# Weight sums by subtraction and by an accumulating DMA, low halves last, and one block summed in PSUM, in a two-layer trunk

## The chip, the cores and the metric

The kernel runs on one core of a Trainium2 chip. The metric is the device time of one launch in microseconds (us). The kernel before took 1077.22 us, the median of three runs (1075.41, 1077.22 and 1082.15). The five engines of the core, TensorE (PE), VectorE (DVE), ScalarE (ACT), GpSimd (POOL) and SyncE (SP), each work through a list of instructions in order and wait for each other by semaphores. DMAs are issued from SP's and POOL's lists.

## The reference

The model has two layers on an input of 512 rows by 1024 columns, all float32. Each layer has three groups of attention-like heads behind one projection, and then a feed-forward part; only the latter is touched here:

```python
    x = x + jnp.concatenate([ya, yb, yc], axis=-1) @ w_out
    u = _rms(x, norm2) @ w_ff1
    return x + jnp.square(jax.nn.relu(u)) @ w_ff2
```

`w_ff1` is 1024 by 4096 and `w_ff2` 4096 by 1024.

## The kernel before

**Products of split numbers.** Each float32 weight block is split into a high half, written by ScalarE (`whi`, L203), and a low half, which VectorE gets as the block less its high half (`wlo`, L204). The activations are split alike. A matmul pair then becomes three: high by high, high by low, low by high (`mm3`, L260 to 263). Splits of weights go through three buffer pairs (`HIB = 3`), so a split can start when the product three back has been read out by TensorE.

**Seven products for eight.** The feed-forward part of a layer (L1090 to 1343) runs the first two of eight ff1 row groups plainly (`ff1_std`), and the other six in a Strassen/Winograd form (`ff1_st`, L1219): the weight is cut into blocks A11, A12, A21, A22, and seven products are made with A11, S1 = A21 + A22, S2 = S1 + A11, A12, S4 = S2 + A12, S3 = A11 + A21 and A22, in the order A11, S1, S2, A12, S4, S3, A22 (L47; signs are put into the stored blocks). ff2 does the same in eight groups (`ff2`, L1277): four steps s with two column halves dg each, whose products alternate. Here ff1 groups are called a2 to a7, ff2 groups b0.0, b0.1, b1.0, to b3.1. `ff_pairs` (L117) interleaves them one by one: a b product, then an a product, for 84 products; the last 14 are b products alone (b3.0 and b3.1). A b group so has its own next product four products later and an a group two later, and in the last 14 a b group's is two later. Each product is 24 matmuls of 128 by 128 weights with 256 moving columns.

**Operands.** Weights are loaded into 128x1024 buffers, three `raw` and four `fraw`, handed out in rings in the order of the products (`load_ahead`, `take`, `drop`): a load can start when an earlier job gives its buffer back. A one-block operand is a plain DMA from SP's list (L156). For the sums of two blocks from HBM (S1 and S3), SP loads the first and POOL issues a DMA that adds the second while it is written (L158). S2 and S4 are summed by VectorE into A11's buffer (L214, L218).

**Outputs.** `ff1_st` adds products in PSUM banks and by VectorE: block (0,0) is the first product, which ScalarE copies to the SBUF tile `ct`, plus another product, added by VectorE (L1233). ScalarE then makes relu squared in `ct`; `csplit`, `gsplit`, `n1_`, `n2_` and `tail_` (L1164 to 1190) form the sums and splits of the activations that ff2 needs, in the tiles `gx`, `yg`, `xhl`. `acc` (L1257) adds each ff2 product from its bank into the running sum `xT` (L1265).

**What sets the order.** The code states the work in the order of the products; the framework's scheduler then puts each engine's instructions in a fixed order, weighing when it believes each one to be ready. So the place of an instruction in an engine's list isn't that of its line in the code, and a wait in the list holds up all that stands behind it.

Of the kernel before, what the change touches and what calls it, by code (L numbers as in the profile page):

```python
# [15 lines left out]
AF = mybir.ActivationFunctionType  # L16
ALU = mybir.AluOpType
AX = mybir.AxisListType

P = 128  # L20
# [30 lines left out]
def trunk(ctx, tc, x, cols, rows, gate_w, tabs, w_in, w_out, w1, w2, out):  # L51
    nc = tc.nc
    V, A, G, T = nc.vector, nc.scalar, nc.gpsimd, nc.tensor
# [31 lines left out]
    def wt(tag, name):  # L85
        n, bufs = phase["tags"][tag]
        return phase["pool"].tile([P, n], F32, tag=tag, name=nm(name), bufs=bufs)
# [4 lines left out]
    def smt(n, name):  # L92
        return sm.tile([P, n], F32, tag=f"sm{n}", name=nm(name))

    def v3(a, d=HD):
        return a.rearrange("p (h d) -> p h d", d=d)
# [12 lines left out]
    def st_group(l, blocks):  # L109
        grp = {}  # L110
        for which, ij in (("A11", ((0, 0),)), ("S1", ((1, 0), (1, 1))), ("S2", ()), ("A12", ((0, 1),)), ("S4", ()),
                          ("S3", ((0, 0), (1, 0))), ("A22", ((1, 1),))):
            grp[which] = {"ap": [blocks[i, j] for i, j in ij], "which": which, "grp": grp, "n": 4, "w": 256, "ff": l,
                          "gate": None, "parts": 1}
        return grp
# [51 lines left out]
    def drop(jb):  # L167
        jb["ring"].append(jb.pop("raw"))
# [12 lines left out]
    def hilo():  # L181
        hi = wp.tile([P, D], F32R, tag="whi", name=nm("whi"), bufs=HIB)
        lo = wp.tile([P, D], F32R, tag="wlo", name=nm("wlo"), bufs=HIB)
        return hi, lo

    def prep_part(jb, part):
        if "hl" not in jb:
            jb["hl"] = hilo()
        hi, lo = jb["hl"]
        n, w, raw = jb["n"], jb["w"], jb["raw"]  # L190
        W = w
        if jb["gate"] is not None:
            l, k0 = jb["gate"]
            W = 268
            h3, l3, r3 = v3(hi[:, :n * W], W), v3(lo[:, :n * W], W), v3(raw[:, :n * w], w)
            A.activation(h3[:, :, :w], r3, AF.Copy)
            V.tensor_copy(h3[:, :, w:], gws[l][0][:, k0:k0 + n, :])
            V.tensor_tensor(l3[:, :, :w], r3, h3[:, :, :w], ALU.subtract)
            V.tensor_copy(l3[:, :, w:], gws[l][1][:, k0:k0 + n, :])
        else:  # L200
            m = n * w // jb["parts"]
            cs_ = slice(part * m, (part + 1) * m)
            A.activation(hi[:, cs_], raw[:, cs_], AF.Copy)  # L203
            V.tensor_tensor(lo[:, cs_], raw[:, cs_], hi[:, cs_], ALU.subtract)  # L204
        if part == jb["parts"] - 1:
            jb["res"] = [(hi[:, q * W:(q + 1) * W], lo[:, q * W:(q + 1) * W]) for q in range(n)]
            if jb["which"] in (None, "S3", "A22"):
                drop(jb)

    def prep_job(jb):  # L210
        which, g = jb["which"], jb.get("grp")
        if which == "S2":
            a = jb["raw"] = g["A11"]["raw"]
            V.tensor_tensor(a, g["S1"]["raw"], a, ALU.add)  # L214
            drop(g["S1"])
        elif which == "S4":
            a = jb["raw"] = g["A11"]["raw"]
            V.tensor_tensor(a, g["A12"]["raw"], a, ALU.add)  # L218
            drop(g["A12"])
        for part in range(jb["parts"]):  # L220
            prep_part(jb, part)
        if which == "S4":
            drop(g["A11"])

    def prep_ahead(i):
        while pos["prep"] < len(jobs):
# [11 lines left out]
    def getjob():  # L238
        i = pos["get"]
        if i > 0:  # L240
            jobs[i - 1].pop("res", None)
        load_ahead(i)
        prep_ahead(i)
        pos["get"] += 1
        return jobs[i]["res"]
# [14 lines left out]
    def mm3(o, sh, sl, mh, ml, first, last, skip=False):  # L260
        T.matmul(o, sh, mh, start=first, stop=False, skip_group_check=skip)  # L261
        T.matmul(o, sh, ml, start=False, stop=False, skip_group_check=skip)  # L262
        T.matmul(o, sl, mh, start=False, stop=last, skip_group_check=skip)  # L263
# [132 lines left out]
    def headrms(zt, nh, name):  # L396
        sq = wt("tmp", "hsq")
        A.activation(sq[:, :nh * HD], zt, AF.Square)
        ss = smt(nh, name)
        V.tensor_reduce(ss, v3(sq[:, :nh * HD]), AX.X, ALU.add)  # L400
        v = smt(nh, name + "v")
# [42 lines left out]
    for l in range(L):  # L444
        last = l == L - 1
# [288 lines left out]
        def runA():  # L734
# [7 lines left out]
            def s1(c):  # L742
# [8 lines left out]
                for r in range(2):  # L751
                    V.tensor_reduce(v3(mx, 2)[:, :, r], v3(sc[r], 256)[:, :, :nk], AX.X, ALU.max)
                nmx = smt(4, "nmx")
# [321 lines left out]
        ct, bt = 0, 0  # L1075
# [19 lines left out]
        ct = v3(wt("ct", "ct"), S)  # L1095
# [11 lines left out]
        def bank():  # L1107
            return banks.popleft()
# [16 lines left out]

        def prod(bk, bh, bl, start):
            ws = getjob()
            for kk in range(4):
                hi, lo = ws[kk]
                for f in range(2):  # L1130
                    c = slice(f * P, (f + 1) * P)
                    mm3(bk[:, f * 256:(f + 1) * 256], hi[:, c], lo[:, c], bh(kk), bl(kk), start and kk == 0 and f == 0,
                        kk == 3 and f == 1, True)

        def prod1(bk, op, start=True):
            bh, bl = xop(op, 0), xop(op, 1)
            prod(bk, lambda kk: bh[:, kk, :], lambda kk: bl[:, kk, :], start)
# [37 lines left out]
        def act(a, src, sign):  # L1175
            A.activation(ct[:, a], src, AF.Relu, scale=sign)
            A.activation(ct[:, a], ct[:, a], AF.Square)
# [39 lines left out]
                    yield  # L1217

        def ff1_st(s, rr):  # L1219
            X = bank()  # L1220
            prod1(X, 0)
            A.activation(ct[:, 0], X, AF.Copy)
            yield
            Z = bank()
            prod1(Z, 3)
            A.activation(ct[:, 3], Z, AF.Copy)
            yield
            prod1(X, 4, False)
            A.activation(ct[:, 1], X, AF.Copy)
            yield  # L1230
            Y = bank()
            prod1(Y, 1)
            V.tensor_tensor(ct[:, 0], Y, ct[:, 0], ALU.add)  # L1233
            banks.append(Y)
            act(0, ct[:, 0], 1.0)
            csplit(s, rr)
            yield
            prod1(Z, 2, False)
            V.tensor_tensor(ct[:, 1], Z, ct[:, 1], ALU.add)
            banks.append(Z)  # L1240
            act(1, ct[:, 1], 1.0)
            n1_()
            yield
            prod1(X, 5, False)
            V.tensor_tensor(ct[:, 3], X, ct[:, 3], ALU.add)
            act(3, ct[:, 3], -1.0)
            n2_(s, rr)
            yield
            prod1(X, 6, False)
            act(2, X, -1.0)  # L1250
            banks.append(X)
            tail_(s, rr)
            yield
# [23 lines left out]
        def ff2(s):  # L1277
# [18 lines left out]
            for dg in range(2):  # L1296
                Y = bank()
                prod2(Y, s, 1)
                acc(s, dg, 0, 0, Y, True)
                banks.append(Y)  # L1300
# [102 lines left out]
```

## Time and profile before

| | |
|---|---|
| three runs | 1075.41, 1077.22, 1082.15 us |
| profiled execution | 1074.93 us, its span 1073.2 us |
| TensorE (PE) busy | 1059.1 us, 99% |
| VectorE (DVE) busy | 911.9 us, 85% |
| ScalarE (ACT) busy | 626.4 us, 58% |
| GpSimd (POOL) busy | 103.8 us, 10% |
| read from HBM | 147.86 MB |
| accumulating DMAs issued by POOL for weights | 56 |

The span is the time from the first to the last instruction in the trace; the time of the run is a little longer. In a row of the groups by line stand the line, the engine, the operation, the tile written and the tiles read, the count, then busy time and the mean of one in ns, and then the idle time just before and what ended it. In a row of the timeline stand start, duration (both in us), engine, line and operation, and in brackets the idle time ahead of it. A row of the waits has the total in us, how many, and the longest. In the chain a row has its start and its share of the time up to the next piece. The instructions of TensorE overlap each other, so their starts tell the pace, not their durations; the same goes for VectorE, where one starts about 0.08 us before the end of the one ahead.

### The profile page before, as it was taken

How to read it: one execution, taken by the hardware profiler on the slowest of the kernel's cores; microseconds unless marked ns; L12 is line 12 of the kernel's file. 1: busy time of each engine (PE TensorE's matmuls, PEld its weight loads, DVE VectorE, ACT ScalarE, POOL GpSimd, SP SyncE). 2: the span in 40 equal slices, each digit the busy share in tenths (PEclk: the TensorE clock that was granted, in tenths of full speed). 3: DMA queues.
4: the chain of work that ended last, by engine and by line, in shares of the span. 5: the costliest groups of instructions: out<-in, count | busy, mean ns of one | idle time of the engine just before them, and what ended most of it. 6: DMA issues, size and time to landing. Idle time of an engine off the chain costs nothing.

```text
span 1073.2 us, 20903 instructions
## 1 busy us (share of the span) xinstructions
PE 1059.1 (99%) x8376; PEld 989.8 (92%) x8376; DVE 911.9 (85%) x1550; ACT 626.4 (58%) x1097; POOL 103.8 (10%) x154
## 2 busy tenths in 40 slices
PE   8999999999999999999999999999999999999998
PEld 8999977887999999999999998778789999999998
DVE  6696877899997997988977878688999889799897
ACT  5446655376666566566454567444765665576662
POOL 2030020101010010010001200101000100000100
PEclk8999999999999999999999999999999999999999
DMA  6533121145478588588435321213334866876872
GB/s 200 164 110 109 59 68 50 62 174 118 118 197 215 140 213 209 149 210 223 108 108 155 102 80 41 86 44 136 112 87 141 233 178 172 219 183 191 211 185 99
DMA packets 47346, 151.81 MB, mean 141 GB/s; under 512 B 5632, under 2 KB 8832, under 8 KB 47248
## 3 DMA queue, kind: packets, MB, share of 16 engines
q1 hardware_dynamic: 39184, 121.10, 33.8%
q0 software_dynamic: 8064, 29.36, 16.2%
q8 instruction: 66, 1.08, 0.4%
q14 instruction: 32, 0.26, 0.1%
HBM read 147.86 MB, written 2.13 MB: 140 GB/s over the span
## 4 chain that ended last, share of the span: by engine, by line
PE 80%; DVE 11%; ACT 3%; DMA 3%; issue 1%; SPq 0%; DVEq 0%; POOLq 0%
PE at L261 24%; PE at L263 24%; PE at L262 24%; DMA raw<-in_w_dram 3%; DVE wlo L204 2%; DVE rt L719 2%; PE at L849 1%; PE at L891 1%; PE at L874 1%; ACT whi L203 1%; ACT pe L762 1%; PE at L972 1%; DVE yg L1168 1%; DVE z L715 1%; DVE z L721 1%
## 5 line engine op out<-in xcount | busy, mean ns | idle before, releaser
L203 ACT ACTIVATE whi<-raw 128x1024 fp32r<-128x1024 f32 (+1 forms) x144 | 150.9, 1048 | 143.7 <-PE at L262 103.2
L204 DVE TENSOR_TENSOR wlo<-raw,whi 128x1024 fp32r<-128x1024 f32 (+1 forms) x144 | 173.8, 1207 | 41.2 <-ACT whi L203 40.7
L203 ACT ACTIVATE whi<-fraw 128x1024 fp32r<-128x1024 f32 x122 | 129.2, 1060 | 92.4 <-PE at L262 76.2
L261 PE MATMUL at<-yg,whi 128*128 128x256 f32 (+1 forms) x592 | 179.8, 307 | 0.0
L263 PE MATMUL at<-yg,wlo 128*128 128x256 f32 (+1 forms) x592 | 178.4, 301 | 0.0
L262 PE MATMUL at<-xhl,whi 128*128 128x256 f32 (+1 forms) x576 | 177.9, 309 | 0.0
L262 PE MATMUL at<-yg,whi 128*128 128x256 f32 (+1 forms) x560 | 169.6, 303 | 0.0
L261 PE MATMUL at<-whi,xhl 128*128 128x256 f32 (+1 forms) x576 | 164.1, 285 | 2.1 <-ACT whi L203 1.3
L262 PE MATMUL at<-wlo,xhl 128*128 128x256 f32 (+1 forms) x576 | 161.5, 280 | 0.3 <-DVE wlo L204 0.3
L263 PE MATMUL at<-whi,xhl 128*128 128x256 f32 (+1 forms) x576 | 161.5, 280 | 0.0
L261 PE MATMUL at<-xhl,whi 128*128 128x256 f32 (+1 forms) x512 | 161.1, 315 | 0.0
L263 PE MATMUL at<-xhl,wlo 128*128 128x256 f32 (+1 forms) x512 | 160.3, 313 | 0.0
L204 DVE TENSOR_TENSOR wlo<-fraw,whi 128x1024 fp32r<-128x1024 f32 x122 | 148.9, 1221 | 8.6 <-ACT whi L203 8.1
L261 PEld LDWEIGHTS at<-yg,whi 128*128 128x128 f32 x592 | 111.2, 188 | 5.6 <-issue 1.7
L263 PEld LDWEIGHTS at<-yg,wlo 128*128 128x128 f32 x592 | 111.2, 188 | 5.3
L262 PEld LDWEIGHTS at<-xhl,whi 128*128 128x128 f32 x576 | 108.0, 188 | 7.6 <-issue 0.5
L261 PEld LDWEIGHTS at<-whi,xhl 128*128 128x128 f32 x576 | 109.4, 190 | 3.2 <-ACT whi L203 1.6
L262 PEld LDWEIGHTS at<-wlo,xhl 128*128 128x128 f32 x576 | 109.5, 190 | 0.5 <-DVE wlo L204 0.5
L263 PE MATMUL at<-xbx,wlo 128*128 128x256 f32 x384 | 106.6, 278 | 3.4 <-DVE wlo L204 3.4
L263 PEld LDWEIGHTS at<-whi,xhl 128*128 128x128 f32 x576 | 109.3, 190 | 0.3 <-DVE xhl L328 0.3
L262 PEld LDWEIGHTS at<-yg,whi 128*128 128x128 f32 x560 | 105.3, 188 | 4.2 <-DVE yg L1002 0.5
L261 PE MATMUL at<-xbx,whi 128*128 128x256 f32 x384 | 106.1, 276 | 0.0
(286 smaller groups left out, 2423.1 us busy)
## 6 DMA issues: line engine op xcount, KB each, us to landing
fraw<-in_w_dram SPq DMA_DIRECT2D x90, 512.0 KB, 4.5
raw<-in_w_dram SPq DMA_DIRECT2D x66, 512.0 KB, 4.5
raw<-in_w_in_dram SPq DMA_DIRECT2D x34, 512.0 KB, 3.4
fraw<-in_w_dram POOLq DMA_DIRECT2D x34, 512.0 KB, 6.0
raw<-in_w_dram POOLq DMA_DIRECT2D x22, 512.0 KB, 7.9
raw<-in_w_out_dram SPq DMA_DIRECT2D x16, 512.0 KB, 3.4
rowb<-drow SPq DMA_DIRECT2D x16, 256.0 KB, 4.0
raw<-in_w_in_dram SPq DMA_DIRECT2D x12, 256.0 KB, 3.8
```

Source lines behind the costliest of these rows:

```text
L203: A.activation(hi[:, cs_], raw[:, cs_], AF.Copy)
L204: V.tensor_tensor(lo[:, cs_], raw[:, cs_], hi[:, cs_], ALU.subtract)
L261: T.matmul(o, sh, mh, start=first, stop=False, skip_group_check=skip)
L262: T.matmul(o, sh, ml, start=False, stop=False, skip_group_check=skip)
L263: T.matmul(o, sl, mh, start=False, stop=last, skip_group_check=skip)
L715: V.tensor_tensor(z10, z10, bc(rq), ALU.mult)
L719: V.tensor_tensor(r10[:, oo:oo + n, a:a + 32], z10[:, oo:oo + n, b:b + 32], tb(S_, n, a, a + 32), ALU.mult)
L721: V.tensor_tensor(zaq[t], ro[:, :640], rt[:, :640], ALU.add)
L762: A.activation(pe[:, u, :nk], sc[u % 2][:, (u // 2) * 256:(u // 2) * 256 + nk], AF.Exp, bias=nmx[:, u:u + 1], accum_out=ssum[:, u:u + 1])
L849: T.matmul(sp[:, :nk], qTB[rs, pr, n * P:(n + 1) * P], kTB[rs, pr, :nk], start=True, stop=False)
L874: T.transpose(pt[:, b * P:(b + 1) * P], scs[r][:, b * P:(b + 1) * P], ident)
L891: T.matmul(pobs[pr][r * 64:(r + 1) * 64, n * P:(n + 1) * P], zbv[b][:, h * 64:(h + 1) * 64], ps[r][:, b * P:(b + 1) * P], start=b == 0, st ...
```

## The change

- S3 is formed as S2 - A22: only A22 is loaded, and VectorE subtracts it from S2 in A11's buffer (L222). A22's own product then uses the buffer already loaded, with no load.
- S4 is formed in A12's buffer: when A12 has been split, POOL issues an accumulating DMA from SBUF to SBUF (L229) that adds S2 to it. No VectorE sum is left for S4.
- A product (`prod`) runs its 16 matmuls with the high halves first (with the high and the low half of the moving side), then the 8 with the low halves. Before, the three kinds alternated.
- Block (0,0) of `ff1_st` is summed in PSUM: ScalarE copies the first product's bank X to a bank Y, and the other product accumulates there. The VectorE add is gone; Y is held from the group's start.

```diff
-                          ("S3", ((0, 0), (1, 0))), ("A22", ((1, 1),))):
+                          ("S3", ((1, 1),)), ("A22", ())):
...
-        n, w, raw = jb["n"], jb["w"], jb["raw"]
+        n, w, raw = jb["n"], jb["w"], jb.get("src", jb.get("raw"))
...
-            if jb["which"] in (None, "S3", "A22"):
+            if jb["which"] is None:
                 drop(jb)
...
     def prep_job(jb):
         which, g = jb["which"], jb.get("grp")
-        if which == "S2":
-            a = jb["raw"] = g["A11"]["raw"]
-            V.tensor_tensor(a, g["S1"]["raw"], a, ALU.add)
-            drop(g["S1"])
-        elif which == "S4":
-            a = jb["raw"] = g["A11"]["raw"]
-            V.tensor_tensor(a, g["A12"]["raw"], a, ALU.add)
-            drop(g["A12"])
+        last = None
+        if which:
+            a = g["A11"].get("raw")
+            jb["src"] = a if which in ("S2", "S3") else jb["raw"] if "raw" in jb else None
+            if which == "S2":
+                V.tensor_tensor(a, g["S1"]["raw"], a, ALU.add)
+                drop(g["S1"])
+            elif which == "S4":
+                jb["src"], last = g["A12"]["raw"], g["A12"]
+            elif which == "S3":
+                V.tensor_tensor(a, a, jb["raw"], ALU.subtract)
+                last = g["A11"]
+            elif which == "A22":
+                jb["src"], last = g["S3"]["raw"], g["S3"]
         for part in range(jb["parts"]):
             prep_part(jb, part)
-        if which == "S4":
-            drop(g["A11"])
+        if which == "A12":
+            nc.gpsimd.dma_start(jb["raw"], a, accum_op=ALU.add)
+        if last:
+            drop(last)
...
             ws = getjob()
-            for kk in range(4):
-                hi, lo = ws[kk]
-                for f in range(2):
-                    c = slice(f * P, (f + 1) * P)
-                    mm3(bk[:, f * 256:(f + 1) * 256], hi[:, c], lo[:, c], bh(kk), bl(kk), start and kk == 0 and f == 0,
-                        kk == 3 and f == 1, True)
+            for i in range(2):
+                for kk in range(4):
+                    for f in range(2):
+                        c, o = slice(f * P, (f + 1) * P), bk[:, f * 256:(f + 1) * 256]
+                        w = ws[kk][i][:, c]
+                        T.matmul(o, w, bh(kk), start=start and i == kk == f == 0, stop=i == 1 and kk == 3,
+                                 skip_group_check=True)
+                        if i == 0:
+                            T.matmul(o, w, bl(kk), start=False, stop=False, skip_group_check=True)
...
     def ff1_st(s, rr):
-            X = bank()
+            X, Y = bank(), bank()
             prod1(X, 0)
-            A.activation(ct[:, 0], X, AF.Copy)
+            A.activation(Y, X, AF.Copy)
...
-            Y = bank()
-            prod1(Y, 1)
-            V.tensor_tensor(ct[:, 0], Y, ct[:, 0], ALU.add)
+            prod1(Y, 1, False)
+            act(0, Y, 1.0)
             banks.append(Y)
-            act(0, ct[:, 0], 1.0)
```

The change moves instructions on VectorE. Two places follow. The first is where b1.0 begins in layer 0 (with a4): `wlo_630` is the low half of b1.0's A11, `wlo_632` of a4's A11, `wlo_634` of b1.1's A11; `raw1_74` holds b1.0's A11. Lines from L210 on have other numbers after the change (L1183, L1184, L1168 and L1265 are L1194, L1195, L1179 and L1274). Before:

```order
L204 TENSOR_TENSOR wlo_630_4138<-raw1_74,whi_629_4137 128x1024 [waits DMAHW5_50,DVE_50,Activation_50]
L1183 SCALAR_TENSOR_TENSOR ct_527_2865<-ct_527_2865 128x512 [waits DVE_50,Activation_50]
L1184 TENSOR_TENSOR ct_527_2865<-ct_527_2865 128x512
L1265 TENSOR_TENSOR xT_89<-xT_89,at_544_2964 128x2x256 [waits PE_50]
L204 TENSOR_TENSOR wlo_632_4168<-fraw_528_2866,whi_631_4167 128x1024 [waits DMAHW4_50,Activation_50]
L1168 TENSOR_TENSOR gx_526_2864<-ct_527_2865,gx_526_2864 128x1024 [waits Activation_50]
L214 TENSOR_TENSOR fraw_528_2866<-fraw_528_2866 128x1024 [waits DMASW0_50,DVE_50]
L204 TENSOR_TENSOR wlo_634_4203<-fraw_528_2866,whi_633_4202 128x1024 [waits DMAHW6_50,PE_50,Activation_50]
L214 TENSOR_TENSOR raw1_74<-raw2_75,raw1_74 128x1024 [waits DMASW1_50]
```

And now:

```order
L204 TENSOR_TENSOR wlo_630_4132<-raw1_74,whi_629_4131 128x1024 [waits DMAHW0_50,DVE_50,Activation_50]
L217 TENSOR_TENSOR raw1_74<-fraw_528_2866,raw1_74 128x1024 [waits DMASW1_50,DVE_50]
L1194 SCALAR_TENSOR_TENSOR ct_527_2865<-ct_527_2865 128x512 [waits Activation_50]
L1195 TENSOR_TENSOR ct_527_2865<-ct_527_2865 128x512
L1274 TENSOR_TENSOR xT_89<-xT_89,at_545_2965 128x2x256 [waits PE_50]
L1179 TENSOR_TENSOR gx_526_2864<-ct_527_2865,gx_526_2864 128x1024 [waits Activation_50]
L204 TENSOR_TENSOR wlo_632_4162<-fraw_528_2866,whi_631_4161 128x1024 [waits DMAHW1_50]
L204 TENSOR_TENSOR wlo_634_4197<-fraw_528_2866,whi_633_4196 128x1024 [waits DMAHW2_50,PE_50,Activation_50]
```

The S2 sum of b1.0, which waits for POOL's accumulating DMA of S1 (DMASW1), stood behind three splits and now stands behind the first of them. The same holds for b2.0 and for both groups in layer 1.

The second place is S4 of a4, in layer 0. `wlo_644` is the low half of a4's A12, `wlo_646` of b1.0's S2, `wlo_648` of a4's S4. Before, with the sum for S4 of a4 in the first row and that of b1.0 (L218, `raw1_74`) in the fifth:

```order
L218 TENSOR_TENSOR fraw_528_2866<-raw0_73,fraw_528_2866 128x1024 [waits DMAHW2_50,DVE_50]
L1265 TENSOR_TENSOR xT_89<-xT_89,at_541_2961 128x2x256 [waits PE_50]
L204 TENSOR_TENSOR wlo_644_4351<-raw0_73,whi_643_4350 128x1024 [waits Activation_50]
L204 TENSOR_TENSOR wlo_646_4381<-raw1_74,whi_645_4380 128x1024 [waits PE_50,Activation_50]
L218 TENSOR_TENSOR raw1_74<-raw2_75,raw1_74 128x1024 [waits DMAHW4_50,DVE_50]
L1265 TENSOR_TENSOR xT_89<-xT_89,at_542_2962 128x2x256 [waits PE_50]
L204 TENSOR_TENSOR wlo_648_4412<-fraw_528_2866,whi_647_4411 128x1024 [waits Activation_50]
```

And now:

```order
L1274 TENSOR_TENSOR xT_89<-xT_89,at_542_2962 128x2x256 [waits PE_50]
L204 TENSOR_TENSOR wlo_644_4344<-raw2_75,whi_643_4343 128x1024 [waits DMAHW6_50,Activation_50]
L204 TENSOR_TENSOR wlo_646_4375<-raw1_74,whi_645_4374 128x1024 [waits PE_50,Activation_50]
L222 TENSOR_TENSOR fraw_528_2866<-fraw_528_2866 128x1024 [waits DMAHW0_50,DMASW3_50]
L1274 TENSOR_TENSOR xT_89<-xT_89,at_545_2965 128x2x256 [waits PE_50]
L204 TENSOR_TENSOR wlo_648_4405<-raw2_75,whi_647_4404 128x1024 [waits Activation_50]
```

The sums for S4 are gone. S3's subtraction (L222) stands ahead of S4's split and waits for the new DMA (DMASW3), since it overwrites the S2 that this DMA reads.

## The prediction

> **What bounds the kernel now.** I read the page's busy line first, then the waits and the groups by line (shapes kept apart), then the timelines of TensorE and VectorE and the chain where a wait ends. One row of each of the first three:
>
> ```profile
> PE 1059.1 (99%) x8376; PEld 989.8 (92%) x8376; DVE 911.9 (85%) x1550; ACT 626.4 (58%) x1097; POOL 103.8 (10%) x154
> ```
> ```profile
> PEld at L263 <- DVE wlo L204: 4.3, 5, 1.2
> ```
> ```profile
> L263 PE MATMUL at<-xbx,wlo 128*128 128x256 f32 x384 | 106.6, 278 | 3.4 <-DVE wlo L204 3.4
> ```
>
> TensorE is busy for 99% of the span, so work removed elsewhere gives nothing unless TensorE waits for it. In the feed-forward part it waits for low halves of weights (`wlo`), 4.3 us in five waits, nearly all at products with `xbx`, the ff1 group's S1. The first of layer 0, on TensorE, VectorE, the chain and POOL in turn:
>
> ```profile
> 354.36 0.28 PE L261 MATMUL at<-yg,whi 128*128 128x256 f32 x1
> ...
> 355.04 0.28 PE L261 MATMUL at<-xbx,whi 128*128 128x256 f32 x1
> 355.15 0.28 PE L262 MATMUL at<-xbx,whi 128*128 128x256 f32 x1
> 356.48 0.39 PE L263 MATMUL at<-xbx,wlo 128*128 128x256 f32 x1 [1.05 <-DVE wlo L204]
> ```
> ```profile
> 334.79 1.22 DVE L204 TENSOR_TENSOR wlo<-raw,whi 128x1024 fp32r<-128x1024 f32 x1
> ...
> 342.62 1.23 DVE L204 TENSOR_TENSOR wlo<-raw,whi 128x1024 fp32r<-128x1024 f32 x1 [0.29 <-ACT whi L203]
> 343.80 0.69 DVE L1183 SCALAR_TENSOR_TENSOR ct<-ct 128x512 f32<-128x512 f32 x1
> 344.41 0.68 DVE L1184 TENSOR_TENSOR ct<-ct 128x512 f32<-128x512 f32 x1
> 345.01 0.68 DVE L1265 TENSOR_TENSOR xT<-xT,at 128x512 f32<-128x512 f32 x1
> 345.61 1.22 DVE L204 TENSOR_TENSOR wlo<-fraw,whi 128x1024 fp32r<-128x1024 f32 x1
> 346.75 1.22 DVE L1168 TENSOR_TENSOR gx<-ct,gx 128x1024 fp32r<-128x1024 f32 x1
> ...
> 351.73 1.23 DVE L214 TENSOR_TENSOR raw<-raw,raw 128x1024 f32<-128x1024 f32 x1 [1.33 <-DMA raw<-in_w_dram]
> ...
> 355.20 1.22 DVE L204 TENSOR_TENSOR wlo<-fraw,whi 128x1024 fp32r<-128x1024 f32 x1
> ```
> ```profile
> 336.04 4.39 DMA raw<-in_w_dram
> ...
> 341.02 10.68 DMA raw<-in_w_dram
> ```
> ```profile
> 337.89 0.87 POOL L158 DMA_DIRECT2D fraw<-in_w_dram  x1 [16.55 <-DMA fraw<-in_w_dram]
> ```
>
> Six matmuls from 354.36 to 355.04, high and low ones, are 0.1133 us each, so a product of 24 is 2.72 us. The S1 product of group a4 starts at 355.04. Its third matmul, the first low one, is due at 355.27 and starts at 356.48, when the low half split at 355.20 is there: 1.2 us lost. That split was late because VectorE stood until 351.73 for the S1 operand of b1.0: its plain load took from 336.04 to 340.43, and the accumulating DMA behind it, issued at 341.02 while another one (337.89) was under way, 10.68.
>
> **The change, part by part.**
>
> *Low products last.* The low half is wanted after 16 matmuls (1.81 us) instead of 2 (0.23). All stalls above are 1.2 us or less and lie inside the 1.58 gained: -4.3 us. Count and size of the matmuls stay and the spacing above is over high and low ones alike, so TensorE's own work is 0. The high half is read out 8 matmuls (0.9 us) earlier, so ScalarE may split, and loads behind it may start, up to 0.9 us sooner.
>
> *Block (0,0) in PSUM.*
>
> ```profile
> L1233 DVE TENSOR_TENSOR ct<-at,ct 128x512 f32<-128x512 f32 x12 | 8.3, 691 | 3.6 <-PE at L263 3.5
> ```
>
> Twelve VectorE adds go, 8.3 us of VectorE, none on the path: none stands between the waited-for DMA and the late split. ScalarE's copy stays and writes a bank in place of `ct`, and eight banks still suffice. No row shows such a copy; it is followed by products of other banks, which cover it: 0, ±1.
>
> *S3 by a subtraction, A22 without a load.* Loads per group fall from 7 to 5, 56 of 512 KB over the 28 groups, and one VectorE sum stands where one stood (L222 for L218, both 128x1024). The stall shown ends at an accumulating DMA, not at a plain load, so the bytes saved buy nothing but quicker DMAs for the rest: 0.
>
> *S4 by an accumulating DMA.*
>
> ```profile
> raw<-in_w_in_dram SPq DMA_DIRECT2D x34, 512.0 KB, 3.4
> fraw<-in_w_dram POOLq DMA_DIRECT2D x34, 512.0 KB, 6.0
> raw<-in_w_dram POOLq DMA_DIRECT2D x22, 512.0 KB, 7.9
> ```
> ```profile
> DMA to landing us min/median/max: 5.2/6.7/10.7
> ```
>
> In an ff1 group S4 is two products after A12 (in ff2 groups four, but two in a layer's last pair). The DMA can go when A12's low half is done. A low half ends 3.03 us ahead of its product: the one of 342.62 ends at 343.85, and its product starts three products (8.16) before 355.04, at 346.88. From there to S4's low matmuls are 3.03 + 2×2.72 + 1.81 = 10.28 us. After the landing VectorE has, in its new order, S3's subtraction (1.14 start to start, as 345.61 to 346.75), an add into xT (0.60) and S4's split (1.22), 2.96 in all. So the DMA has 7.3 us, 8.2 with the earlier release. The medians are 6.0 and 7.9, and in ff1 groups no second accumulating DMA follows within two products: 0. In the last pair of each layer two follow closely, and 10.7 would cost 2.5 for each of four: I take 0.5, bounds 0 and 10. No row shows a DMA from SBUF to SBUF; those from HBM bound it, and a longer one everywhere is a rival. [...]
>
> *The order on VectorE*, the largest term. In ff2 groups s=1 and s=2 of each layer the first S2 sum (L217, was L214) moves to right behind the split of b1.0's (b2.0's) A11, ahead of the two ct steps, an add into xT, the gx split and the split of a4's (a6's) A11. It still needs the S1 operand, whose load still starts when a3.S3 (split at 334.79) gives its buffer back. If that lands as before, VectorE stands from 343.85 to 351.73, 7.9 us, with all these behind it, and TensorE waits for the last. Start to start they take 1.14 + 0.61 + 0.60 + 0.60 + 1.14, and the split 1.22, so it ends at 351.73 + 5.31 = 357.04. Its product starts two products before 355.04, at 349.60, and wants it at 351.41: **5.6 us late**. The other three places, VectorE and then POOL:
>
> ```profile
> 412.29 1.22 DVE L204 TENSOR_TENSOR wlo<-raw,whi 128x1024 fp32r<-128x1024 f32 x1
> ...
> 429.19 1.23 DVE L214 TENSOR_TENSOR raw<-raw,raw 128x1024 f32<-128x1024 f32 x1 [1.34 <-DMA raw<-in_w_dram]
> ```
> ```profile
> 864.33 1.22 DVE L204 TENSOR_TENSOR wlo<-raw,whi 128x1024 fp32r<-128x1024 f32 x1
> ```
> ```profile
> 942.13 1.22 DVE L204 TENSOR_TENSOR wlo<-raw,whi 128x1024 fp32r<-128x1024 f32 x1
> ...
> 957.48 1.23 DVE L214 TENSOR_TENSOR raw<-raw,raw 128x1024 f32<-128x1024 f32 x1 [0.90 <-DMA raw<-in_w_dram]
> ```
> ```profile
> 869.41 0.89 POOL L158 DMA_DIRECT2D raw<-in_w_dram  x1 [2.10 <-DMA raw<-in_w_dram]
> ```
> ```profile
> DMA to landing us min/median/max: 6.0/7.0/8.0
> ```
>
> From the end of the split that frees the buffer to the landing it was 15.7 us at the first place (336.01 to 351.73), 15.7 at the second (413.51 to 429.19), 11.9 at the third (865.55 to 869.41 + 8.0) and 14.1 at the fourth (943.35 to 957.48). Being in time takes 10.1, so 5.6, 5.6, 1.8 and 4.0 us late, **17 us**, is the upper end. The lower end is 0: a plain load and an accumulating DMA at their quickest (3.4 and 5.2, with 0.6 between as from 340.43 to 341.02) land after 9.2. I stay nearer the upper end, because the transfers that share these microseconds (S1 of a4, b1.0 and b1.1, A12 of a4) are all still there and start at the same points; only some queued ahead of them go. I take 0.9 off each place for the earlier release and 0.9 for the shorter queue: 3.8 + 3.8 + 0 + 2.2, **about 10 us**.
>
> Sum: -4.3 + 10 + 0.5 = +6.2. The profiled execution took 1074.93 us, 1.73 more than its span and 2.3 less than the median of the three runs (1077.22). On its scale the result is 1081.1; between the two scales I say 1082.
>
> **Rivals.**
>
> *A. The S1 operand lands in time.* With 56 loads gone, a landing 10 to 11 us after the split leaves at most 0.9 us at each place: -4.3 + 0 to 3.6, 1070.6 to 1074.2. For it: the third place, at 11.9 already. Against: the two at 15.7, where two accumulating DMAs overlap.
>
> *B. It lands as late as before, or the clock falls too.* -4.3 + 17 + 0.5: 1088.1, slower. It decides where the landing stays over 14 us after the split.
>
> ```profile
> 10.00:15.00 5.00, 5.00 (x24) 4.84 (x23) 4.76 (x10) 5.00 (x11) 0.00 (x0) 0.51 0.84 304
> 15.00:20.00 5.00, 5.00 (x47) 5.00 (x45) 5.00 (x10) 4.42 (x9) 0.69 (x1) 1.00 0.43 123
> ```
>
> At the kernel's start the granted clock is 0.51 (24 matmuls in 5 us), then 1.00; the pauses above, up to 1.2 us, are too short to show what one of 4 or 5 us does. [...]
>
> *C. S4's DMA is late in every ff1 group.* At 10 us to landing, 1.8 too long in 12 groups: +22, so 1093, or 1103 with the S2 term. For it: 10.68 above. Against: nothing accumulates beside it there.
>
> *D. TensorE's own spacing changes* with two matmuls in a row on one high half. 2×98 products of 2.72 us are 533 us; 2% of that is 10.7 us, up or down. Against it: the even spacing above.
>
> **Chances and numbers.** Forecast (1076 to 1087) 0.45; A 0.25; B 0.17, a third of it with the clock; C 0.08; D 0.05. The range 1070 to 1094 leaves out C's larger half, B's end with the clock, and D. A measurement tells about 1% (10.8 us) from no change. Faster by more needs 1066.4, more than all stalls removed: 0.03, from D. Slower (over 1088): B, C, the rest of D and the forecast's edge, 0.32. Within: 0.65.
>
> **What would show it.** Right: no wait of TensorE for `wlo` at S1 products of ff1 groups; VectorE idle 5 to 7 us on a DMA ahead of L217 at the four places, and TensorE idle 2 to 4 us at the first low matmul of a4.A11 and a6.A11; HBM reads down by 29 MB (56 × 0.524); L229's DMAs landing in 5 to 8 us, without a wait at S4. Wrong: L217 waiting under 3 us (A); waits at S4's low matmuls in most ff1 groups (C); a granted clock under 1.00 behind a stall (B with the clock); a spacing other than 0.113 us (D).

## The result: 1.038 times the time before

The kernel after took 1119.91 us, the median of six runs (1115.54 to 1122.38), beside 1076.32 us before (six runs, 1071.60 to 1082.15). The ratio is 1.0382, 95% interval 1.0342 to 1.0422. By the medians it is 44 us slower, where 1082 in a range up to 1094 was forecast. The profiled execution took 1119.46 us, its span 1117.7.

First the busy row and the HBM row of the page, then TensorE's waits and two of VectorE's, and the group of matmuls that the longest waits belong to:

```profile
PE 1077.2 (96%) x8376; PEld 1006.8 (90%) x8376; DVE 899.6 (80%) x1538; ACT 621.7 (56%) x1097; POOL 102.6 (9%) x154
...
HBM read 118.50 MB, written 2.13 MB: 108 GB/s over the span
```
```profile
PE at L1141 <- DVE wlo L204: 22.0, 4, 6.6
PE at L1141 <- DVE xT L1274: 5.4, 2, 3.4
PE at L1141 <- ACT whi L203: 2.7, 5, 0.7
...
DVE raw L217 <- DMA raw<-in_w_dram: 18.9, 4, 8.4
DVE raw L217 <- DMA fraw<-in_w_dram: 17.3, 2, 8.9
```
```profile
L1141 PE MATMUL at<-xhl,wlo 128*128 128x256 f32 x352 | 52.1, 289 | 22.0 <-DVE wlo L204 22.0
```

The S1 stalls of before (3.4 us at `xbx,wlo`) are gone, and 29.4 MB less is read. In their place stand four waits of 5.5 us on average for a low half, at `xhl,wlo`: A11 of a4 and of a6, in both layers. They are the four places that the prediction named, and VectorE's waits at L217 (36 us, 33 of them at these places, 7.0 to 8.9 us each) are the cause it named, though both are longer than it said. TensorE is also 18 us longer busy with the same 8376 matmuls. The first place, in windows of 5 us (busy time and count of PE, PEld, DVE, ACT, POOL, then the granted clock, the DMA share and GB/s):

```profile
345.00:350.00 5.00, 4.22 (x38) 4.02 (x36) 0.45 (x1) 0.00 (x0) 0.00 (x0) 1.00 1.05 224
350.00:355.00 5.00, 0.09 (x1) 0.09 (x1) 5.00 (x7) 3.52 (x5) 0.00 (x0) 0.72 0.05 11
355.00:360.00 5.00, 5.00 (x27) 5.00 (x28) 5.00 (x6) 4.09 (x5) 0.00 (x0) 0.60 0.00 0
360.00:365.00 5.00, 5.00 (x47) 5.00 (x46) 5.00 (x6) 2.03 (x3) 0.00 (x0) 1.00 0.55 163
```

VectorE stands first (0.45 us busy), TensorE then pauses (one matmul), and behind the pause the clock is at 0.60: 27 matmuls in 5 us, where it otherwise does some 44 to 47. The first 17 behind this pause start some 213 ns apart, beside 113.3 in the trace of before. This slower running is called half clock below. There is a third loss, which the granted clock does not show:

```profile
1030.00:1090.00 60.00, 60.00 (x511) 60.00 (x511) 48.91 (x54) 32.00 (x39) 4.36 (x5) 1.00 0.53 140
```

At clock 1.00 the matmuls start 117.8 ns apart here, not 113.3. (A window also counts the two or three matmuls that only overlap its edges, so its count gives a slightly smaller number.)

To put sizes to the three, the starts of the 4704 matmuls of the seven-product part (2 × 98 products) were taken from each trace: a gap of over 250 ns to the next is a pause, 190 to 250 is half clock, 114.5 to 135 is slow spacing, and of each gap what exceeds 113.3 ns is summed. (The first matmul behind a pause mostly falls into the half clock band too, some 0.1 us each.) At 113.3 ns throughout the part would be 533 us.

| us | pauses | half clock | slow spacing | the part in all |
|---|---|---|---|---|
| before | 4.0 | 1.0 | 1.1 | 539.2 |
| after | 32.7 | 11.4 | 7.6 | 585.1 |

The part is 45.9 us longer and the span 44.5, so nearly all of the loss lies in this part.

### The profile page after: what moved, and what is told of

It reads as the page before. It is cut to its first block, busy times and chain, and to the rows that moved or that the text cites. A ratio compares the mean times of both kernels' runs of the same rounds, so it can differ in the third digit from the quotient of the medians.

```text
span 1117.7 us, 20838 instructions
## 1 busy us (share of the span) xinstructions
PE 1077.2 (96%) x8376; PEld 1006.8 (90%) x8376; DVE 899.6 (80%) x1538; ACT 621.7 (56%) x1097; POOL 102.6 (9%) x154
## 3 DMA queue, kind: packets, MB, share of 16 engines
q0 software_dynamic: 8064, 29.36, 14.6%
## 4 chain that ended last, share of the span: by engine, by line
PE 53%; DVE 19%; DMA 15%; issue 9%; ACT 3%; POOL 0%; SPq 0%; DVEq 0%; POOLq 0%; ACTq 0%
PE at L1141 14%; PE at L269 9%; PE at L271 8%; PE at L270 8%; DVE wlo L204 7%; PE at L1144 7%; DMA raw<-in_w_dram 6%; DMA fraw<-in_w_dram 3%; DMA fraw<-fraw 2%; DVE rt L727 2%; DVE xT L1274 1%; DMA raw<-raw 1%; PE at L857 1%; PE at L899 1%; DMA fraw<-raw 1%
## 5 line engine op out<-in xcount | busy, mean ns | idle before, releaser
L204 DVE TENSOR_TENSOR wlo<-raw,whi 128x1024 fp32r<-128x1024 f32 (+1 forms) x150 | 181.3, 1210 | 20.5 <-ACT whi L203 20.3
L203 ACT ACTIVATE whi<-fraw 128x1024 fp32r<-128x1024 f32 x116 | 121.2, 1053 | 95.8 <-DMA fraw<-fraw 26.4
L204 DVE TENSOR_TENSOR wlo<-fraw,whi 128x1024 fp32r<-128x1024 f32 x116 | 140.3, 1221 | 9.8 <-ACT whi L203 9.5
L1141 PE MATMUL at<-yg,whi 128*128 128x256 f32 x464 | 113.5, 283 | 6.1 <-DVE xT L1274 5.4
L1144 PE MATMUL at<-yg,whi 128*128 128x256 f32 x432 | 105.3, 281 | 0.0
L1144 PE MATMUL at<-xhl,whi 128*128 128x256 f32 x416 | 100.3, 281 | 0.0
L1141 PEld LDWEIGHTS at<-yg,whi 128*128 128x128 f32 x464 | 89.3, 193 | 6.6 <-issue 5.8
L1141 PE MATMUL at<-gx,whi 128*128 128x256 f32 x368 | 91.1, 284 | 1.7 <-ACT whi L203 1.7
L1141 PE MATMUL at<-xbx,whi 128*128 128x256 f32 x384 | 90.6, 278 | 0.0
L1144 PE MATMUL at<-xbx,whi 128*128 128x256 f32 x384 | 90.6, 278 | 0.0
L1141 PE MATMUL at<-xhl,whi 128*128 128x256 f32 x352 | 84.9, 281 | 0.4 <-ACT whi L203 0.4
L1144 PE MATMUL at<-gx,whi 128*128 128x256 f32 x336 | 83.5, 285 | 0.0
L1144 PEld LDWEIGHTS at<-yg,whi 128*128 128x128 f32 x432 | 82.9, 192 | 0.0
L1144 PEld LDWEIGHTS at<-xhl,whi 128*128 128x128 f32 x416 | 79.5, 191 | 0.0
L1274 DVE TENSOR_TENSOR xT<-xT,at 128x512 f32<-128x512 f32 x112 | 76.5, 683 | 3.3 <-PE at L1141 3.0
```

The source lines that it names most:

```text
L1141: T.matmul(o, w, bh(kk), start=start and i == kk == f == 0, stop=i == 1 and kk == 3, skip_group_check=True)
L1144: T.matmul(o, w, bl(kk), start=False, stop=False, skip_group_check=True)
L1274: V.tensor_tensor(t_, t_, q2(bk), ALU.subtract if i else ALU.add)
```

## The experiments

Twelve kernels were run. Ratios are to the kernel before, timed on the same chip in the same set; the right-hand columns are the sums just described.

| kernel | median us | ratio, 95% interval | pauses | half clock | slow spacing |
|---|---|---|---|---|---|
| lo_last | 1098.82 | 1.0253 (1.0214 to 1.0292) | 15.3 | 8.2 | 7.3 |
| sums_only | 1116.83 | 1.0424 (1.0384 to 1.0463) | 32.4 | 11.2 | 6.6 |
| late_s2 | 1092.57 | 1.0192 (1.0154 to 1.0231) | 9.6 | 3.6 | 10.1 |
| lo_late | 1068.91 | 0.9961 (0.9933 to 0.9989) | 0.5 | 0.1 | 1.6 |
| lo_psum_late | 1068.53 | 0.9927 (0.9895 to 0.9960) | 0.2 | 0.1 | 0.1 |
| s4_dve | 1071.67 | 0.9934 (0.9901 to 0.9968) | 2.1 | 0.3 | 0.3 |
| tail_dve | 1086.14 | 1.0077 (1.0042 to 1.0112) | 7.8 | 2.1 | 8.0 |
| ladder | 1143.07 | one run | 54.3 | 11.7 | 9.3 |
| pair_dve | 1088.42 | 1.0126 (1.0072 to 1.0179) | 9.0 | 1.3 | 2.3 |
| after_s4dve | 1091.01 | 1.0159 (1.0105 to 1.0213) | 13.8 | 5.1 | 4.5 |
| a37_dve | 1071.51 | 0.9992 (0.9961 to 1.0024) | 2.4 | 0.4 | 0.1 |
| psum00 | 1076.88 | 1.0024 (0.9998 to 1.0049) | 2.5 | 0.3 | 10.2 |

The kernel before has a median of 1070.7 to 1080.2 in these sets, and the runs that the ratios use lie between 1069 and 1084. So two kernels of different sets are better compared by their own times. The sums are those of one profiled execution each. That of pair_dve took 1080.78 us, its shortest run (the other three took 1088 to 1090), and that of psum00 1081.49.

### Which edit makes the four stalls

**lo_last** is the kernel before with the new `prod` and nothing else.

> The kernel before with one edit: low products last in prod. Loads, sums and block (0,0) are those of before. On VectorE the edit alone moves the S2 sum (L214) of b1.0 and b2.0 right behind the split of their A11. Theory 1 (the order on VectorE, then the half clock behind a long stall): four stalls of about 5.5 us at a4.A11 and a6.A11, about 2 us each of half clock behind them, less the 4.3 us of S1 stalls: +22 + 8 - 4 = +26, ratio 1.02 to 1.03. Theory 2 (S4's DMA in SBUF and the load pattern cost the time): none of that is in here, so the S1 stalls go and the ratio is 0.996. Theory 3 (two matmuls on one high half are slower): products longer than 2.72 us everywhere, no waits.

1.0253 is inside the range of theory 1, in part by luck: the four stalls are 13.6 us where 22 were expected, and 7.3 us of slow spacing, which the expectation did not have, make up for it. TensorE waits 13.6 us for low halves, in four waits, at the same four products, and no load or sum differs from before. What moved the S2 sum on VectorE is the order of TensorE's matmuls alone, by way of the scheduler.

```profile
PE at L1133 <- DVE wlo L204: 13.6, 4, 3.9
```

**lo_late** is lo_last with each S2 sum queued on VectorE behind the low split of the product four ahead:

```diff
-            V.tensor_tensor(lo[:, cs_], raw[:, cs_], hi[:, cs_], ALU.subtract)
+            los[pos["prep"]] = V.tensor_tensor(lo[:, cs_], raw[:, cs_], hi[:, cs_], ALU.subtract)
...
-            V.tensor_tensor(a, g["S1"]["raw"], a, ALU.add)
+            with tc.issue_after(los[pos['prep'] - 4].ins):
+                V.tensor_tensor(a, g["S1"]["raw"], a, ALU.add)
```

> The kernel before with low products last and the S2 sums queued behind the low split of the product four ahead. Theory 1: the S1 stalls (4.3 us) go and nothing comes: ratio 0.993 to 0.997. If half of lo_last's loss stays, theory 1 is wrong and the low-last order itself costs it (theory 3).

Measured 0.9961 (0.9933 to 0.9989): the four stalls are gone, the S1 stalls too, and the part takes 535.2 us. One edge of the order was worth 30 us (1098.82 to 1068.91). That also ends theory 3, that TensorE is slower with two matmuls in a row on one high half.

**late_s2** puts the same edge into the kernel after.

> The kernel after with one more edit: each S2 sum is queued on VectorE behind the low split of the product four ahead of it, so it can't stand in front of the ct steps and splits while its S1 operand is under way. Theory 1: the four long stalls (22 us) and the half clock behind them (about 9) go; the stalls in the last products of each layer (12 us) stay: 1119.9 - 31 = 1089, ratio 1.01. Theory 2: nothing of the DMAs changes, ratio 1.035. Theory 3: ratio 1.035 less the stalls, with products over 2.72 us.

1092.57, 27 us less, where 31 were expected: the four stalls and their half clock are gone, but 1.0192 remains. Of the 21 us by which the part is longer than lo_late's, 9 are pauses and 12 half clock and slow spacing. So theory 1 was right on the stalls and is not the whole.

**sums_only** is the kernel after with the old `prod` and the old block (0,0).

> The kernel after without the low-last order and without block (0,0) in PSUM: only the sums and loads are changed. The S2 sums stand where they stood before. Theory 1: no stall at a4.A11 and a6.A11, the stalls in the last 14 products of each layer (12 us after) stay in part, and some S4 of ff1 groups are up to 1 us late since the low half is wanted 1.58 us earlier: +5 to +15, ratio 1.005 to 1.014. Theory 2: most of the 43 us, ratio 1.03 to 1.04. Theory 3: ratio 1.00 or below.

This was missed by far: 1.0424 where 1.005 to 1.014 stood. The stalls at a4.A11 and a6.A11 were absent as expected; the time goes in many small waits, by groups of TensorE:

```profile
L271 PE MATMUL at<-xbx,wlo 128*128 128x256 f32 x384 | 107.5, 280 | 9.3 <-DVE wlo L204 9.2
L271 PE MATMUL at<-gx,wlo 128*128 128x256 f32 x368 | 102.8, 279 | 2.2 <-DVE wlo L204 2.2
L271 PE MATMUL at<-xhl,wlo 128*128 128x256 f32 x352 | 102.4, 291 | 7.9 <-DVE wlo L204 7.9
L269 PE MATMUL at<-xhl,whi 128*128 128x256 f32 x352 | 102.0, 290 | 4.0 <-ACT whi L203 4.0
```

The first row is S1 in ff1 groups, which got worse (3.4 before), the others are mostly S4's. The new sums alone, without the low-last order, cost 46 us. With the low-last order and the S2 sums held back they cost 24 (late_s2 beside lo_late), so that order hides about half; without the edge it brings the four stalls. So the two parts do not add: 28 us for one, 46 for the other, 44 together.

### What S4's DMA does

The time to landing of after's DMAs from SBUF to SBUF, from the view of line L229, is about what the prediction bounded from those out of HBM. But VectorE stands for them, at S3's subtraction L222 (waits of VectorE in after):

```profile
DMA to landing us min/median/max: 4.5/5.3/8.3
```
```profile
DVE raw L222 <- DMA raw<-raw: 20.5, 6, 4.3
...
DVE fraw L222 <- DMA fraw<-fraw: 15.4, 4, 5.6
...
DVE raw L222 <- DMA fraw<-raw: 7.7, 2, 4.4
DVE fraw L222 <- DMA raw<-fraw: 5.9, 2, 3.2
```

That is 49.5 us in 14 waits, 3.5 each. **s4_dve** is late_s2 with this sum on VectorE, into A12's buffer, at the time of S4's split:

```diff
                 jb["src"], last = g["A12"]["raw"], g["A12"]
+                V.tensor_tensor(jb["src"], jb["src"], a, ALU.add)
...
-        if which == "A12":
-            nc.gpsimd.dma_start(jb["raw"], a, accum_op=ALU.add)
```

> late_s2 with S4 summed by VectorE into A12's buffer instead of by the DMA from SBUF to SBUF, in all 28 groups; S3 by subtraction and A22 without a load stay. late_s2 still loses 22 us to lo_late: 9.5 of pauses, 3.6 of half clock, 10.7 of products that run at 118 ns a matmul. Theory (S4's DMA: VectorE stands at S3's subtraction and S4's split until it lands): the pauses in the last products go, ratio 1.000 to 1.006. Rival (the pattern of loads: S3's block of the second column half comes into the buffer that S4 gives back, four products ahead): the pauses at b0.1's S3 and the last S3 stay, ratio 1.010 to 1.020.

1071.67 us, 21 less than late_s2, though VectorE has 28 sums more. Pauses fall from 9.6 to 2.1 us and the slow spacing from 10.1 to 0.3. The loads from HBM are the same in both, so which blocks are loaded is not the cause. (The ratio of 0.993 is to a set in which the kernel before was at 1080; against lo_late's 1068.91 it is 3 us slower.)

Where does the DMA cost? **tail_dve** has VectorE sum S4 in the last ff2 pair of each layer only (`s == NS - 1`), **pair_dve** in the first and the last (`s in (0, NS - 1)`), **a37_dve** in the last and in a3 and a7.

> late_s2 with S4 by VectorE in the last ff2 pair of each layer alone (four sums), the DMA in the other 24 groups. Theory: the pauses from b3.0's S2 to b3.1's A22 (5.1 us in layer 0, 1.0 in layer 1, and 2.7 of half clock) go, those at b0.1's S3 (3.0 us) stay: 1092.6 - 8 = 1084, ratio 1.011 to 1.014. Rival (the last pauses come from the xT adds queued on VectorE, not from the DMA): ratio 1.018 to 1.020.

1086.14, six of the 21 us, near the time expected. The pauses of the last products did not all go, though: some 4.5 of 6.1 us remain, most of them in layer 1, where no DMA of S4 runs any more. Why is open.

> late_s2 with S4 by VectorE in the first and the last ff2 pair of each layer (s=0 and s=3), the DMA in the other 20 groups, the twelve ff1 groups among them. Theory (only those DMAs cost whose landing holds up a buffer or the last products; a pause at b0.1's S3 then starts the 118 ns spacing): the pauses at b0.1's S3 go, and with them the slow spacing behind: 1071 to 1076 us. Rival (each S4 DMA in ff1 groups costs too, or the slow spacing has nothing to do with a pause): 1080 or above, as tail_dve's 1086.

Missed: 1088.42, no better than tail_dve. The trace shows why the pause counted to b0.1's S3 did not go: it stands behind that product's last matmul and ahead of the first one of a3's S4, whose high half waits for a3's own DMA, which this kernel keeps (TensorE's timeline, then the chain there, in layer 1):

```profile
865.98 0.39 PE L1145 MATMUL at<-xhl,whi 128*128 128x256 f32 x1 [1.54 <-ACT whi L204]
```
```profile
858.56 6.21 DMA fraw<-fraw
...
864.87 1.06 ACT whi L204
```

The pauses at a3's S4 are 2.0 of the 9.0 us in this trace. Nearly all of the other 7 lie in the last products, where VectorE already makes S4.

> late_s2 with S4 by VectorE in a3, a7 and the last ff2 pair of each layer, the DMA in the other 20 groups (b0.0 to b2.1, a2, a4, a5, a6). The pause that pair_dve kept stands at the end of b0.1's S3, that is, ahead of the first matmul of a3's S4, whose high half waits for a3's own DMA. Theory (the DMA costs where VectorE is behind when A12 is split, which is at a3 and in the last groups, and nothing elsewhere): 1069 to 1075 us and no pause at a3's S4. Rival (every S4 DMA delays buffers by holding VectorE, so pauses turn up at other places): 1080 or above.

1071.51, as good as s4_dve, with the DMA still in 20 of 28 groups. VectorE still stands 30 us for these DMAs at S3's subtraction, in eight waits, and nothing of it shows in the time. So the loss comes from the other eight at most, those at a3, a7 and the last pair. At a3 and in part of the last pair VectorE splits A12 late: in late_s2 the DMA goes 0.2 to 0.9 us ahead of A12's product at a3, 0.2 to 2.8 in the last pair, and 1.8 to 3.3 in the other ff1 groups. S4's split and S3's subtraction stand behind it. At a7 the DMA is not late (2.4 and 3.1 us), and a7 was changed only together with a3, so its share is not known. The chain of after shows the effect at the first of the four places, from a3's S4 DMA on:

```profile
323.11 5.29 DMA fraw<-fraw
328.40 0.02 issue
328.42 1.22 DVE fraw L222
...
333.72 1.15 DVE wlo L204
334.87 0.02 issue
334.88 4.41 DMA fraw<-in_w_dram
...
339.91 9.55 DMA fraw<-in_w_dram
...
349.55 1.22 DVE raw L217
...
353.64 1.23 DVE wlo L204
```

a3's DMA holds VectorE until 328.42, so the split that gives b1.0's S1 its buffer ends at 334.87, and the operand lands at 349.46. **after_s4dve** is the kernel after, with its four stalls, but with S4 by VectorE:

> The kernel after with S4 by VectorE in all groups; the S2 sums stand where they stand after, ahead of the ct steps and splits at the four places. Theory (S4's DMA ahead of the four places holds VectorE, the buffer for b1.0's S1 comes back later, and so the four stalls are 22.6 us after but 15 with low products last alone): the four stalls fall to 14 to 17 us, 8 of half clock behind them, and 0 to 8 of slow spacing: 1094 to 1103. Rival (the stalls are as long with or without that DMA, since the loads set them): 22 us of stalls, 1104 to 1112.

1091.01 us, under the 1094 to 1103 expected. The pauses at the four products are 2.5, 3.0, 3.9 and 2.4 us, 12 in all and even under the 14 to 17 expected, beside 22.7 after by the same measure. So S4's DMA and the place of the S2 sum make these stalls together: with the DMA alone (late_s2) there are none, with the place alone 12 to 14 us. Whether the DMA does it by VectorE's wait or also by its traffic is not told apart here; the chain above shows the wait.

### The pause, the clock and the spacing

**ladder** is lo_late with twelve pauses made on purpose, by repeating one low split; the product's result is the same. It asks how long a pause has to be for half clock to follow.

```diff
+            for _ in range({42: 12, 56: 10, 70: 8, 84: 7, 98: 6, 112: 5, 182: 5, 196: 6, 210: 7, 224: 8, 238: 10, 252: 12}.get(pos["prep"], 1)):
```

> lo_late with twelve deliberate pauses of TensorE: the low split of one product is repeated 12, 10, 8, 7, 6 and 5 times in layer 0 (14 products apart) and 5, 6, 7, 8, 10 and 12 times in layer 1, each repeat 1.14 us of VectorE; the result of the split is the same. The first 4 to 5 repeats are covered. [...] Also to be seen: whether the spacing of 118 ns begins and ends at pauses.

Single pauses of 1.27, 1.86, 1.86, 1.87 and 2.03 us left the clock alone; pauses of 2.53, 3.80, 4.02, 7.57 and 10.21 us were each followed by matmuls at 213 ns, at a cost of 1.3 to 1.7 us (2.8 with the pauses behind, after the longest). One of 1.93 us had 1.1 us of it behind, and what came after others was broken up by further pauses. So half clock follows the long pauses and not the shortest, and the edge is near 2 us in this trace. The pause of 2.53 us, then the one of 2.03, in windows of 4 us with the columns of before:

```profile
893.00:897.00 4.00, 1.64 (x11) 1.44 (x10) 3.68 (x4) 2.52 (x4) 0.00 (x0) 0.87 0.50 170
897.00:901.00 4.00, 4.00 (x27) 4.00 (x27) 3.55 (x5) 1.20 (x3) 0.00 (x0) 0.71 0.68 231
416.00:420.00 4.00, 4.00 (x38) 4.00 (x37) 4.00 (x5) 0.60 (x1) 1.56 (x2) 1.00 0.70 112
420.00:424.00 4.00, 2.14 (x18) 1.94 (x18) 4.00 (x4) 2.01 (x2) 0.00 (x0) 1.00 1.03 245
424.00:428.00 4.00, 4.00 (x36) 4.00 (x36) 4.00 (x5) 2.34 (x3) 0.00 (x0) 1.00 0.42 141
```

After 2.53 us the clock falls to 0.71 (27 matmuls in 4 us), after 2.03 it stays at 1.00. The other traces show that the length alone does not decide. All single pauses of 3.0 us and more were followed by half clock. Those of 2.21 us in after and 2.25 in tail_dve were too, but those of 2.36 in after_s4dve, 2.41 in sums_only and 2.60 in pair_dve were not. Here is the one of 2.21 us in after, then that of 2.60 in pair_dve:

```profile
1104.00:1106.00 2.00, 0.22 (x2) 0.25 (x3) 2.00 (x4) 0.00 (x0) 0.00 (x0) 1.00 0.21 72
1106.00:1110.00 4.00, 4.00 (x23) 4.00 (x23) 2.66 (x4) 0.00 (x0) 0.00 (x0) 0.57 0.49 164
```
```profile
533.00:536.00 3.00, 0.57 (x5) 0.46 (x4) 3.00 (x5) 2.58 (x4) 0.00 (x0) 1.00 0.00 0
536.00:539.00 3.00, 2.88 (x25) 2.67 (x23) 3.00 (x5) 1.26 (x2) 0.00 (x0) 1.00 0.28 93
```

In sums_only five pauses of 1.5 us were followed by half clock, each with another of 0.7 to 1.3 us just ahead (1.0 to 1.6 us from start to start). Why pauses of like length end differently is open: no run here tells it.

**psum00** is the kernel before with block (0,0) in PSUM only.

> The kernel before with block (0,0) summed in PSUM and nothing else. Theory: covered work goes, the S1 stalls of 4 us stay: ratio 0.997 to 1.002. Rival (VectorE has less to do and the S1 sums come sooner): 0.993 to 0.996, with S1 stalls under 3 us.

1.0024 (0.9998 to 1.0049): no change that can be told. **lo_psum_late** adds the same to lo_late.

> lo_late (the kernel before with low products last and S2 sums held back) plus block (0,0) summed in PSUM. Theory: the twelve VectorE adds were covered, so nothing moves: ratio 0.993 to 0.998, as lo_late's 0.9961. Rival (the copy from bank to bank or the bank held longer makes TensorE wait): 1.000 or above, with a wait for a bank or a copy in ff1 groups.

1068.53 us beside lo_late's 1068.91, with 0.9927 (0.9895 to 0.9960) in its own set. It has the lowest time of these kernels, though it can't be told from lo_late, and its seven-product part, 533.4 us, is at the 533 of unbroken matmuls: there is nothing left to gain in it but matmuls.

psum00's trace is of use for the slow spacing. One pause of 0.8 us stands at a2's S1 at 278 us, and from there to the end of the layer every product runs at 117.8 ns a matmul. (The kernel before has a pause of the same length at the same place and keeps 113.3 behind it, so such a pause does not always bring it.) Two windows of 40 us of psum00, and the first again of lo_psum_late, which has no pause there:

```profile
300.00:340.00 40.00, 40.00 (x342) 40.00 (x342) 32.02 (x35) 24.93 (x30) 4.28 (x5) 1.00 0.77 215
880.00:920.00 40.00, 40.00 (x355) 40.00 (x354) 37.28 (x41) 25.87 (x32) 2.60 (x3) 1.00 0.63 166
```
```profile
300.00:340.00 40.00, 40.00 (x355) 40.00 (x355) 32.25 (x35) 25.19 (x30) 4.33 (x5) 1.00 0.82 221
```

342 matmuls against 355 in the same time, at clock 1.00 and a like DMA load. In the ladder stretches of this spacing mostly begin and end at a pause, but not all do (one begins at 880 us without any): the one from 360 to 385 us has 215 matmuls in 25 us, and there are 220 in the 25 us behind the next pause.

```profile
360.00:385.00 25.00, 25.00 (x215) 25.00 (x214) 24.01 (x25) 14.88 (x18) 2.60 (x3) 1.00 0.62 136
391.00:416.00 25.00, 24.97 (x220) 24.97 (x221) 24.99 (x29) 18.70 (x23) 1.91 (x3) 1.00 0.74 210
```

## Why the prediction was wrong, step by step

**Low products last, -4.3 us: right.** lo_late's pauses are 0.5 us where before's are 4.0.

**The order on VectorE, +10 (0 to 17): the mechanism and the four places were right, the size was not.** 22 us were measured. The step that failed first is the 0.9 us taken off each place "for the earlier release", with the sentence that the load still starts when a3.S3's split gives its buffer back. It does, but that split was itself late. Before it ended 13.6 us ahead of a4.A11's product (336.01 to 349.60); I took 14.5. In after it ended at 334.87 and that product started at 347.24, 12.4 ahead, since a3's S4 DMA had held VectorE till 328.42. In after_s4dve, without that DMA, it ended 14.1 to 14.3 us ahead at the four places, close to what I took. The second failure is in layer 1, where I carried over the quicker landings of before: I had 0 us for the third place, which became the longest wait. All four places in us, what I took and what after shows:

| place | split ends ahead of the product | from the split's end to the landing | TensorE waits |
|---|---|---|---|
| first | 14.5, was 12.4 | 14.8, was 14.6 | 3.8, was 5.7 |
| second | 14.5, was 12.0 | 14.8, was 14.4 | 3.8, was 5.9 |
| third | 14.5, was 11.8 | 11.0, was 14.9 | 0, was 6.6 |
| fourth | 14.5, was 14.0 | 13.2, was 14.5 | 2.2, was 3.8 |

The rest of the step came out as written: from the sum's start to the end of the split that TensorE waits for it was 5.3 us (I had 5.31). By its own sign, a landing over 14 us after the split, rival B came true (I gave it 0.17), and even its 17 us were too few. Why the landings of layer 1 took longer than before is open; in after_s4dve the third took 14.6 us too. after_s4dve and lo_last, in which no DMA of S4 runs, gave 12 and 14 us of pauses, inside my bounds.

**S4 by DMA, +0.5 (0 to 10): wrong, and the costliest miss of reasoning.** The time to landing was bounded rightly and most S4 products were in time, so rival C, all twelve ff1 groups late, did not come. But I asked only whether S4 would be late. I named what stands on VectorE behind the wait (an add into xT and S4's split) and left out what those release: buffers, loads and banks. VectorE stood 49.5 us at L222. That sum is not the price, as a37_dve shows: 30 us of such waits cost nothing there. The edit is worth 21 us in late_s2 (to s4_dve), and it feeds the term above. In the last products of layer 0 VectorE stood 3.2 us at L222 and 1.6 us for the split behind the next S4 DMA, and then worked without a gap up to the xT add at 551.37 that TensorE waited for. TensorE's waits for L1274 are 5.4 us, one in each layer. VectorE's timeline there:

```profile
531.73 0.68 DVE L1274 TENSOR_TENSOR xT<-xT,at 128x512 f32<-128x512 f32 x1
535.60 1.23 DVE L222 TENSOR_TENSOR raw<-raw,fraw 128x1024 f32<-128x1024 f32 x1 [3.19 <-DMA raw<-raw]
...
540.16 1.23 DVE L204 TENSOR_TENSOR wlo<-fraw,whi 128x1024 fp32r<-128x1024 f32 x1 [1.57 <-ACT whi L203]
...
551.37 0.69 DVE L1274 TENSOR_TENSOR xT<-xT,at 128x512 f32<-128x512 f32 x1
```

**The clock, held for a third of rival B: right in kind, and thought too unlikely.** It cost 10.4 us more than before. after has it behind six pauses: the four, and two in the last products (3.5 us in layer 0, 2.2 in layer 1). That it would come, and what it would cost, was my estimate, and no run showed it then: the longest pause of this part before was 1.2 us, and it left the clock at 1.00. after shows 1.6 to 2.2 us behind each of the six.

**TensorE's own spacing (rival D): it did change, for a reason I had not.** Two matmuls on one high half keep 113.3 ns (lo_psum_late). The slow spacing mostly begins at pauses and cost 6.5 us more than before; what brings it is open.

**Block (0,0) and the loads, 0: right** for block (0,0), as far as psum00 and lo_psum_late can tell. The loads and the subtraction for S3 were not changed alone; s4_dve, which has them without S4's DMA, is 3 us above lo_late, so the 29 MB less bought nothing that shows.

Sum: pauses +28.7, half clock +10.4, slow spacing +6.5, together 45.6 us; the part grew by 45.9 and the span by 44.5. The forecast had +5.7 to +6.2 for pauses and none for the others.

## What to carry to other kernels

Price an accumulating DMA between two steps of one in-order engine by what that engine would have released while it waits, not only by whether the DMA's own consumer is in time. The wait itself may cost nothing, as 30 us of it in a37_dve did. When an edit lets an instruction become ready sooner on paper, look at where the scheduler puts it: lo_last lost 28 us and lo_late gained 2 by the same edit, one ordering edge apart. On a kernel at 99% TensorE, count pauses twice: here single pauses of 1.9 to 2.6 us brought the half clock in some cases, those of 3.0 us and more always, and the spacing went from 113.3 to 117.8 ns behind one of 0.5 us in after (at 539.5 us).

## What was not expected of the hardware

- **A second pace of TensorE.** 113.3 and 117.8 ns a matmul of 256 columns, both at a granted clock of 1.00, each held for up to 270 us, with a change mostly at a pause, as small as 0.3 us, and sometimes at none. Why is open: no run tells it. It might also explain the spread of the kernel before (1069 to 1084 us) beside that of lo_late (1068.1 to 1070.5) and lo_psum_late (1068.0 to 1070.1), which hardly pause; that is argued from one profile each, not shown.
- **Half clock behind pauses of some 2 us, but not all of them.** Single pauses of 1.9 to 2.6 us went either way in these traces, those of 3.0 us and more always brought it. The price was 1.3 to 1.7 us in the ladder, for pauses of 2.53 to 7.57 us, and up to 2.7 in other traces, with no clear growth with the pause's length.
- **SBUF to SBUF is only a little faster.** The 28 accumulating DMAs of 512 KB in after took 4.5, 5.3 and 8.3 us (least, median, most), beside 5.2, 6.7 and 10.7 of the 56 out of HBM in the kernel before.
